# One projection pair of a decoder layer moved behind the memory attention, with its softmax shares per chunk

## Chip, cores and metric

The kernel runs on one core of a Trainium2 chip. The metric is the device time of one execution in microseconds (us), the median of several runs. All computation is in float32; a large product is made of three products of rounded parts (high x high, high x low, low x high).

## What is computed

One layer (DEPTH is 1, so the mixer is the dilated window attention) and a final norm, for x of 2048 x 1024 and 256 memory rows:

```python
h = rmsnorm(x, norm_g[i])
proj = h @ w_in[i]
q, k, v = proj[..., :c1], proj[..., c1:c2], proj[..., c2:c3]
qm, gate = proj[..., c3:c4], proj[..., c4:]
mix = dilated_window_mixer(q, k, v)
mo = memory_attention(qm, rmsnorm(mem, mem_norm_g[i]), w_mem_kv[i])
y = jnp.concatenate([mix, mo], axis=-1) * jax.nn.silu(gate)
x = x + y @ w_out[i]
return rmsnorm(x, final_norm_g)
```

The mixer has three groups of four heads, with windows and dilations (128, 1), (512, 4) and (2048, 16). Each head attends to a band of keys in its own residue class, and the three groups' outputs are weighed against each other, per position and head, by the softmax over the groups of their log-sum-exp. These weights are called shares here. Memory attention has four heads over all 256 memory rows.

## The kernel before

**Staging.** Positions are held in 4 chunks of 512. The normalised input stays in SBUF as a rounded part xH and a remainder xL, [128, chunk, 8, 512] each. In the code group 2 is the one with dilation 16. Heads go in pairs, two heads in 128 rows. The main loop (L755) takes the pairs in the order (2,0), (2,1), (1,0), (1,1), (0,0), (0,1); for each pair and chunk it makes four projections, K, V, Q and gate (`proj_k`, `proj_v`, `proj_q`, `proj_gate`), each 24 matmuls at L140 to L142. At the end of a chunk `burst` (L477) issues the values of the chunk before and the scores of this one. Exponentials come with their row sums (`nm_all`, `l_all`); the weights are turned by a VectorE transposition and a round trip through DRAM (`turn_tiles`, L329: one DMA out at L336, four back at L342). The result times its gate goes to a DRAM buffer (`store_z`).

**After the pairs** `memory_kv` has made the memory keys and values, and eight memory units (pair, chunk) follow (L815 to L828): a Q and a gate projection each, then `mem_values` (L444) of the unit two back and `mem_scores` (L455) of this one. Beside them `shares` (L557) turns the row maxima and sums of all heads, sends them to DRAM (`st_dr`), reads them back with 128 lanes, weighs the groups and writes `f_dr`. From the fourth unit on the output weights are loaded over chunks 0 and 1 of xH and xL (`load_wo`, L607), and from the seventh on y for chunk 0 is made over chunk 2 (`make_y`, L621): load z, load the shares of two heads broadcast over 64 rows each, multiply (L638), round (L639), subtract (L640).

**Output.** `out_block` (L654) multiplies 128 positions by the output weights, 48 matmuls of 512 columns in two banks (L669 to L671), adds the residual rows on eviction (L674), and norms. Sixteen blocks follow each other, and during those of chunk c y for chunk c+1 is made. The last two memory units' values are issued after blocks 0 and 2 (L835).

**Order.** A slot is a step of `run` (L706): a fourth of a projection, six matmuls. `at(n, f)` issues f n slots later; `steps` runs a generator one step for each slot. The framework adds the waits, assigns the buffers of a tag and orders each engine's instructions when the kernel is built, starting from the order of the code; it may take an instruction ahead of others that it reckons not ready. So memory values and scores stand among the projections of later units. All DMAs are issued by SP, in one queue. PSUM has three banks for projections and output (`pp`), four for scores (`ps`) and one for values (`po`).

## Time and profile before

| | us |
|---|---|
| median of 3 runs | 997.66 (996.65 to 997.77) |
| the profiled execution, its own time | 999.34 |
| its span from first to last instruction | 997.4 |
| TensorE busy in the span | 965.4 |
| first matmul of the output stage | 777.67 |

Busy times are those of one profiled execution. A line of the code (L669) names the instruction's place; a tile's name (`pp`, `xH`) what it writes and reads. Where an operation waits, the profile names the instruction that released it. Matmuls are pipelined, so one lasts longer than the step from one to the next.

### The profile page before, as it was taken

Reading aid. Unit: us, or ns where it says so; the run is one execution under the profiler, and the core shown is the slowest. Engines: PE = TensorE matmul, PEld = TensorE weight load, DVE = VectorE, ACT = ScalarE, POOL = GpSimd, SP = SyncE. Lnnn points to the kernel's source line nnn. Section 1 sums busy time; section 2 is a strip of 40 time slices with the busy share of each in tenths; the row PEclk is TensorE's granted clock in tenths of the full one; section 3 lists DMA queues with packets and bytes.
Section 4 is the critical chain, followed back from the end, with each engine's and each line's share of the span. In section 5 each row is a group of like instructions: output and inputs, shape, how many; then the busy total and the mean of one; then the engine's idle time right before and its main releaser. Section 6 shows DMA issues by size and latency. Waiting matters only on the chain.

```text
span 997.4 us, 13857 instructions
## 1 busy us (share of the span) xinstructions
PE 965.4 (97%) x4836; PEld 758.1 (76%) x4836; DVE 425.7 (43%) x995; ACT 325.1 (33%) x992; POOL 245.5 (25%) x391
## 2 busy tenths in 40 slices
PE   8899999999999999999999999999999788999997
PEld 6677888887888888877777777787767466788886
DVE  7866333333333333333334334335543544465333
ACT  5755422242223222332233232433232330232111
POOL 4411500050004100321123011245356450011000
PEclk9999999999999999999999999999999889899999
DMA  6465321141224322442345432534475775887311
GB/s 198 153 201 180 128 74 53 54 146 67 74 86 135 124 80 85 131 135 85 95 117 158 118 93 87 174 131 130 120 211 173 219 224 182 270 244 243 117 64 63
DMA packets 102133, 135.17 MB, mean 136 GB/s; under 512 B 29872, under 2 KB 63920, under 8 KB 102064
## 3 DMA queue, kind: packets, MB, share of 16 engines
q1 hardware_dynamic: 102064, 134.30, 43.0%
q8 instruction: 38, 0.62, 0.3%
q14 instruction: 31, 0.25, 0.1%
HBM read 89.14 MB, written 45.12 MB: 135 GB/s over the span
## 4 chain that ended last, share of the span: by engine, by line
PE 82%; issue 2%; DMA 2%; DVE 1%; POOL 1%; ACT 1%; POOLq 0%; SPq 0%; ACTq 0%
PE pp L140 18%; PE pp L142 18%; PE pp L141 18%; PE pp L669 6%; PE pp L670 6%; PE pp L671 6%; PE ps L399 3%; PE po L421 3%; PE ps L455 1%; PE po L444 1%; DMA p<-t_dr 1%; POOL p L471 1%; PE pp L540 1%; DMA wh<-in_xrows 1%; ACT p L464 1%
## 5 line engine op out<-in xcount | busy, mean ns | idle before, releaser
L140 PE MATMUL pp<-xH,wh 128*128 128x512 f32 x888 | 357.2, 403 | 0.0
L142 PE MATMUL pp<-xH,wl 128*128 128x512 f32 x888 | 353.5, 398 | 1.8 <-DVE wl L78 1.8
L141 PE MATMUL pp<-xL,wh 128*128 128x512 f32 x888 | 353.3, 398 | 1.5 <-DVE xL L198 1.5
L140 PEld LDWEIGHTS pp<-xH,wh 128*128 128x128 f32 x888 | 167.8, 189 | 47.6 <-issue 7.7
L142 PEld LDWEIGHTS pp<-xH,wl 128*128 128x128 f32 x888 | 167.5, 189 | 45.3 <-DVE wl L78 3.5
L141 PEld LDWEIGHTS pp<-xL,wh 128*128 128x128 f32 x888 | 167.7, 189 | 42.5 <-DVE xL L198 2.4
L324 POOL COPY vb<-mid 32x128 f32<-32x128 f32 (+1 forms) x208 | 60.1, 289 | 260.2 <-DVE mid L321 252.0
L669 PE MATMUL pp<-xH 128*128 128x512 f32 (+1 forms) x264 | 105.3, 399 | 11.6 <-ACT xH L639 6.4
L324 ACT COPY vb<-mid 32x128 f32<-32x128 f32 (+1 forms) x208 | 60.7, 292 | 168.8 <-DVE mid L321 166.7
L671 PE MATMUL pp<-xH,xL 128*128 128x512 f32 (+1 forms) x264 | 103.5, 395 | 0.7 <-DVE xL L640 0.7
L670 PE MATMUL pp<-xL,xH 128*128 128x512 f32 (+1 forms) x264 | 104.2, 395 | 0.0
L78 POOL TENSOR_TENSOR wl<-wraw,wh 128x512 fp32r<-128x512 f32 x52 | 67.4, 1308 | 142.1 <-ACT wh L77 136.5
L378 ACT ACTIVATE p<-p,nm_all 128x128 f32<-128x128 f32 (+1 forms) x192 | 86.1, 450 | 44.2 <-DVE nm_all L377 28.5
L333 DVE STREAM_TRANSPOSE mid<-p 128x1024 f32<-128x1024 f32 (+1 forms) x56 | 66.9, 1194 | 49.8 <-DMA t_dr<-mid 33.9
L471 POOL TENSOR_SCALAR p<-p,sm 128x256 f32<-128x256 f32 x64 | 62.8, 1000 | 72.0 <-DVE sm L467 54.9
L310 DVE SCALAR_TENSOR_TENSOR tmp<-pp,Rb 128x512 f32<-128x512 f32 x31 | 21.4, 691 | 121.8 <-PE pp L142 121.7
L669 PEld LDWEIGHTS pp<-xH 128*128 128x128 f32 x264 | 51.3, 194 | 25.4 <-ACT xH L639 8.4
L311 ACT ACTIVATE u<-tmp 128x512 f32<-128x512 f32 x29 | 18.2, 629 | 144.9 <-DVE tmp L310 144.6
L671 PEld LDWEIGHTS pp<-xH,xL 128*128 128x128 f32 x264 | 51.3, 195 | 13.5 <-DVE xL L640 2.4
L377 DVE CUSTOM_DVE_ANT_0 p<-ps,nb 128x128 f32<-128x128 f32 (+1 forms) x192 | 57.5, 362 | 7.8 <-PE ps L399 7.6
L670 PEld LDWEIGHTS pp<-xL,xH 128*128 128x128 f32 x264 | 51.5, 195 | 10.3 <-issue 0.4
L249 DVE TENSOR_TENSOR tmp<-pp,Rb 128x512 f32<-128x512 f32 x24 | 16.6, 691 | 82.0 <-PE pp L142 81.9
(137 smaller groups left out, 839.1 us busy)
## 6 DMA issues: line engine op xcount, KB each, us to landing
t_dr<-mid SPq DMA_DIRECT2D x46, 512.0 KB, 3.0
p<-t_dr SPq DMA_DIRECT2D x184, 128.0 KB, 3.3
wraw<-in_w_in SPq DMA_DIRECT2D x56, 256.0 KB, 2.9
wh<-in_xrows SPq DMA_DIRECT2D x16, 512.0 KB, 5.3
out<-wh SPq DMA_DIRECT2D x15, 512.0 KB, 3.1
z_dr<-u SPq DMA_DIRECT2D x29, 256.0 KB, 2.9
Rb<-z_dr SPq DMA_DIRECT2D x24, 256.0 KB, 5.5
tmp<-in_xT SPq DMA_DIRECT2D x22, 256.0 KB, 3.1
```

Of the source, the lines that this page charges most:

```text
L78: on.tensor_tensor(wl, raw, wh.bitcast(F32), op=ALU.subtract)
L140: pe.matmul(ps, wh[:, k, :], xh, start=(k == 0), stop=False)
L141: pe.matmul(ps, wh[:, k, :], xl, start=False, stop=False)
L142: pe.matmul(ps, wl[:, k, :], xh, start=False, stop=(k == NK - 1))
L324: (gp.tensor_copy if (i + j) % 2 else a.copy)(dst[32 * j:32 * j + 32, :, 32 * i:32 * i + 32], mid[32 * i:32 * i + 32, :, 32 * j:32 * j + 32])
L333: v.transpose(mid.rearrange("p (j t b) -> p t j b", j=4, t=n), src.rearrange("p (t j b) -> p t j b", t=n, j=4))
L377: v.tensor_tensor_reduce(p, sc, bias, -SCALE, BIG, ALU.add, ALU.min, nm)
L378: a.activation(p, p, AF.Exp, bias=nm, scale=-1.0, accum_out=l)
L471: gp.tensor_scalar(w, w, sm[:, 1, h, b:b + 1], None, op0=ALU.mult)
L669: pe.matmul(ps, yH[:, k, bs], woH[:, k, ns], start=(k == 0), stop=False)
L670: pe.matmul(ps, yH[:, k, bs], woL[:, k, ns], start=False, stop=False)
L671: pe.matmul(ps, yL[:, k, bs], woH[:, k, ns], start=False, stop=(k == NK - 1))
```

## The change

The second pair of group 2 is taken out of its place behind the first one and comes after the memory attention (in the list of pairs (3,0) stands for the memory units, whose order is now pair by pair). Its weights are loaded during the last three memory units. `shares` is run beside the memory units for all heads but the two of the moved pair, whose rows of group 2 do not exist yet; `chunk_shares` does the same for heads 2 and 3 (of every group) chunk by chunk, one chunk behind the moved pair, with `weigh_groups` in common and in three steps. The output weights are loaded during chunks 1 and 2 of the moved pair (`load_wo`, one each 1.875 slots), y for chunk 0 during its chunk 3. The last two memory units' values are issued in its chunk 0, at slot 6 and at the end. Residual rows are loaded two blocks ahead instead of one. The shares in `make_y` have two staging buffers instead of three.

```diff
--- before.py
+++ after.py
@@ -60,6 +60,8 @@
 
     gp.memset(ones, 1.0)
     gp.memset(mhalf, -0.5)
+    gp.memset(nm_all[:, 2, 2:], 0.0)
+    gp.memset(l_all[:, 2, 2:], 0.0)
 
     main = ExitStack()
     pool = main.enter_context(tc.tile_pool(name="main", bufs=1))
@@ -554,16 +556,35 @@
         yield
 
 
+    def weigh_groups(m, f):
+
+        v.tensor_tensor(f[:, 3, :], m[:, 0, :], m[:, 2, :], op=ALU.min)
+        v.tensor_tensor(f[:, 3, :], f[:, 3, :], m[:, 4, :], op=ALU.min)
+        for g in range(3):
+            v.tensor_tensor(f[:, g, :], f[:, 3, :], m[:, 2 * g, :], op=ALU.subtract)
+        yield
+        a.activation(f[:, :3, :], f[:, :3, :], AF.Exp)
+        yield
+        for g in range(3):
+            v.tensor_tensor(m[:, 2 * g, :], f[:, g, :], m[:, 2 * g + 1, :], op=ALU.mult)
+        v.tensor_tensor(m[:, 0, :], m[:, 0, :], m[:, 2, :], op=ALU.add)
+        v.tensor_tensor(m[:, 0, :], m[:, 0, :], m[:, 4, :], op=ALU.add)
+        v.reciprocal(m[:, 0, :], m[:, 0, :])
+        for g in range(3):
+            v.tensor_tensor(f[:, g, :], f[:, g, :], m[:, 0, :], op=ALU.mult)
+
     def shares():
+
         kk = sb([P, 5 * P], F32, "kk", 2)
         vb = sb([P, 5, P], F32, "vb", 2)
         for i, src in enumerate((nm_all, l_all)):
             for g in range(3):
+                n = 32 if g == 2 else 64
                 pt = pbank()
-                pe.transpose(pt[:64, :P], src[:, g].rearrange("p h b -> p (h b)"), ident)
+                pe.transpose(pt[:n, :P], src[:, g, :n // 16].rearrange("p h b -> p (h b)"), ident)
                 t = (vb[:64, 3 * i + g, :] if 3 * i + g < 5 else kk[:64, :P])
-                v.tensor_copy(t, pt[:64, :P])
-                for h in range(4):
+                v.tensor_copy(t[:n], pt[:n, :P])
+                for h in range(n // 16):
                     dst = st_dr[2 * g + i, h]
                     s = t[16 * h:16 * h + 16, :]
                     if g == 2:
@@ -576,25 +597,42 @@
                                      s.rearrange("b (r i) -> b r i", r=16))
             yield
         q = S // 32
-        m = kk[:, :6 * q].rearrange("p (s n) -> p s n", s=6)
-        sp.dma_start(m, st_dr.rearrange("s h (b n) -> (h b) s n", n=q))
+        m = kk[:64, :6 * q].rearrange("p (s n) -> p s n", s=6)
+        sp.dma_start(m, st_dr[:, :2].rearrange("s h (b n) -> (h b) s n", n=q))
         for _ in range(4):
             yield
-        f = vb.rearrange("p b n -> p (b n)")[:, :4 * q]
-        f = f.rearrange("p (s n) -> p s n", s=4)
-        v.tensor_tensor(f[:, 3, :], m[:, 0, :], m[:, 2, :], op=ALU.min)
-        v.tensor_tensor(f[:, 3, :], f[:, 3, :], m[:, 4, :], op=ALU.min)
-        for g in range(3):
-            v.tensor_tensor(f[:, g, :], f[:, 3, :], m[:, 2 * g, :], op=ALU.subtract)
-        a.activation(f[:, :3, :], f[:, :3, :], AF.Exp)
-        for g in range(3):
-            v.tensor_tensor(m[:, 2 * g, :], f[:, g, :], m[:, 2 * g + 1, :], op=ALU.mult)
-        v.tensor_tensor(m[:, 0, :], m[:, 0, :], m[:, 2, :], op=ALU.add)
-        v.tensor_tensor(m[:, 0, :], m[:, 0, :], m[:, 4, :], op=ALU.add)
-        v.reciprocal(m[:, 0, :], m[:, 0, :])
-        for g in range(3):
-            v.tensor_tensor(f[:, g, :], f[:, g, :], m[:, 0, :], op=ALU.mult)
-        sp.dma_start(f_dr.rearrange("g h (b n) -> (h b) g n", n=q), f[:, :3, :])
+        f = vb.rearrange("p b n -> p (b n)")[:64, :4 * q].rearrange("p (s n) -> p s n", s=4)
+        yield from weigh_groups(m, f)
+        yield
+        sp.dma_start(f_dr[:, :2].rearrange("g h (b n) -> (h b) g n", n=q), f[:, :3, :])
+        yield
+
+    def chunk_shares(c):
+
+        cs = slice(c * CH, (c + 1) * CH)
+        t = tmp()
+        for i, src in enumerate((nm_all, l_all)):
+            pt = pbank()
+            pe.transpose(pt[:32, :P], src[:, 2, 2:].rearrange("p h b -> p (h b)"), ident)
+            v.tensor_copy(t[:32, i * P:(i + 1) * P], pt[:32, :P])
+        yield
+        for i in range(2):
+            for h in range(2):
+                b = 16 * h + 4 * c
+                sp.dma_start(st_dr[4 + i, 2 + h, cs].rearrange("(r n) -> r n", r=4), t[b:b + 4, i * P:(i + 1) * P])
+        q = CH // 32
+        m = t[:64, 2 * P:2 * P + 6 * q].rearrange("p (s n) -> p s n", s=6)
+        f = t[:64, 3 * P:3 * P + 4 * q].rearrange("p (s n) -> p s n", s=4)
+        for _ in range(2):
+            yield
+        for h in range(2):
+            sp.dma_start(m[32 * h:32 * h + 32], st_dr[:, 2 + h, cs].rearrange("s (b n) -> b s n", n=q))
+        for _ in range(3):
+            yield
+        yield from weigh_groups(m, f)
+        yield
+        for h in range(2):
+            sp.dma_start(f_dr[:, 2 + h, cs].rearrange("g (b n) -> b g n", n=q), f[32 * h:32 * h + 32, :3, :])
         yield
 
 
@@ -624,10 +662,9 @@
         cs = slice(c * CH, (c + 1) * CH)
         if not staged:
             kk = sb([P, 5 * P], F32, "kk", 2)
-            vb = sb([P, 5, P], F32, "vb", 2).rearrange("p b n -> p (b n)")
-            staged.append([Rb[:, i * CH:(i + 1) * CH] for i in range(3)] + [vb[:, :CH]])
-            staged.append([sb([P, CH], F32, "wraw", 2), sb([P, CH], F32, "wraw", 2), kk[:, :CH]])
-        t, f = staged[0][k % 4], staged[1][k % 3]
+            staged.append([Rb[:, i * CH:(i + 1) * CH] for i in range(3)] + [kk[:, :CH]])
+            staged.append([sb([P, CH], F32, "wraw", 2) for _ in range(2)])
+        t, f = staged[0][k % 4], staged[1][k % 2]
         sp.dma_start(t, z_dr[k // 2][:, k % 2, cs])
         if k < 6:
             for h in range(2):
@@ -657,8 +694,8 @@
         bs = slice(b * P, (b + 1) * P)
         x_t = residual.pop(r)
         last = r == 15
-        if not last:
-            at(3, lambda: load_rows(r + 1))
+        if r < 14:
+            at(3, lambda: load_rows(r + 2))
         cuts = (0, 512, 768, 1024) if last else (0, 512, 1024)
         ss = sb([P, 6], F32, "ss", 2)
         sq = row_tile("wl")
@@ -751,8 +788,30 @@
 
     mem = {}
     ws = []
-    pairs = [(2, 0), (2, 1), (1, 0), (1, 1), (0, 0), (0, 1)]
+    pairs = [(2, 0), (1, 0), (1, 1), (0, 0), (0, 1), (3, 0), (2, 1)]
+
+    def memory_stage():
+
+        at(20, lambda: steps(shares()))
+        following = []
+        for n in range(8):
+            pp, c = divmod(n, 4)
+            st = {}
+            if n in (5, 6):
+                at(1, lambda t=(11, 17)[n - 5]: following.append(load_w(w_in[t])))
+            run(proj_q(st, 3, c, ws[2 + 2 * pp]))
+            if n == 7:
+                following.append(load_w(w_in[5]))
+            run(proj_gate(st, 3, c, ws[1 + 2 * pp], "nb" if n % 3 == 2 else "u"))
+            if n == 7:
+                following.append(load_w(w_in[25]))
+            burst((st, 3, pp, c), 2)
+        return following
+
     for idx, (g, pp) in enumerate(pairs):
+        if g == 3:
+            ws = memory_stage()
+            continue
         col = 2 * g + pp
         nbs = {}
 
@@ -774,7 +833,7 @@
         else:
             at(7, load_bias)
         following = []
-        if idx < 5:
+        if idx < 4:
             n = 2 * pairs[idx + 1][0] + pairs[idx + 1][1]
             ahead = [6 + n, 12 + n, n, 20 + n]
         else:
@@ -783,9 +842,22 @@
         for c in range(NC):
             st = {}
             pv = prev if g == 0 else None
+            if idx == 6:
+                if c == 0:
+                    at(6, burst)
+                else:
+                    at(3, lambda c=c: steps(chunk_shares(c - 1)))
+                if c == 1:
+                    for i in range(2 * NK):
+                        at(15 * i // 8, lambda i=i: load_wo(i))
+                elif c == 3:
+                    for k in range(NK):
+                        at(2 * k, lambda k=k: make_y(0, k))
+                    for i, fn in ((6, lambda: load_rows(0)), (10, load_gfin), (11, lambda: load_rows(1))):
+                        at(i, fn)
 
             def load_ahead():
-                if c == NC - 1:
+                if c == NC - 1 and idx < 5:
                     t = ahead[len(following)]
                     following.append(load_w(w_in[t]) if t is not None else None)
 
@@ -797,9 +869,9 @@
                     at(14, lambda c=c: spread_r(c + 1))
                     at(17, lambda c=c: spread_r(c + 1))
                 run(proj_k(st, g, c, ws[0], pv, late=4 if (idx, c) == (0, 1) else 0))
-                if (idx, c) == (5, 3):
+                if (idx, c) == (4, 3):
                     steps(memory_kv(mem))
-                elif (idx, c) == (5, 1):
+                elif (idx, c) == (4, 1):
                     steps(memory_squares(mem))
                 load_ahead()
                 run(proj_v(st, g, c, ws[1], pv))
@@ -811,28 +883,14 @@
             burst((st, g, pp, c), 1, nbs[0])
             prev = st
         ws = following
-    at(20, lambda: steps(shares()))
-    for n, (pp, c) in enumerate(((0, 0), (0, 1), (1, 0), (1, 1), (0, 2), (1, 2), (0, 3), (1, 3))):
-        st = {}
-        if n == 3:
-            for i in range(2 * NK):
-                at(4 * i // 3, lambda i=i: load_wo(i))
-        elif n == 6:
-            for k in range(NK):
-                at(2 * k, lambda k=k: make_y(0, k))
-        elif n == 7:
-            at(3, lambda: load_rows(0))
-            at(5, load_gfin)
-        run(proj_q(st, 3, c, ws[2 + 2 * pp]))
-        run(proj_gate(st, 3, c, ws[1 + 2 * pp], "nb" if n % 3 == 1 else "u"))
-        burst((st, 3, pp, c), 2)
+    at(2, lambda: steps(chunk_shares(3)))
     for c in range(NC):
         for b in range(4):
             if c < NC - 1:
                 for i in range(2):
                     at(1 + 3 * i, lambda k=2 * b + i: make_y(c + 1, k))
             run(out_block(c, b))
-            if c == 0 and b in (0, 2):
+            if (c, b) == (0, 0):
                 burst()
     assert not todo, todo
     main.close()
```

## Rows read from the trace of the kernel before

**Rows 1.** The page: busy us by engine; TensorE's share in 40 slices

```profile
PE 965.4 (97%) x4836; PEld 758.1 (76%) x4836; DVE 425.7 (43%) x995; ACT 325.1 (33%) x992; POOL 245.5 (25%) x391
...
PE   8899999999999999999999999999999788999997
```

**Rows 2.** Windows: us; busy (count) of PE, PEld, DVE, ACT, POOL; clock; DMA; GB/s

```profile
765.40:800.00 34.60, 28.45 (x118) 18.46 (x117) 18.11 (x28) 11.13 (x38) 19.33 (x19) 0.83 0.78 219
800.00:825.00 25.00, 21.21 (x88) 15.38 (x88) 11.31 (x20) 8.41 (x24) 11.13 (x10) 0.89 0.76 239
825.00:876.00 51.00, 45.30 (x199) 34.32 (x199) 23.60 (x43) 9.23 (x16) 5.09 (x7) 0.93 0.72 223
876.00:984.00 108.00, 108.00 (x478) 89.41 (x478) 48.66 (x95) 20.49 (x35) 10.67 (x14) 1.00 0.47 152
```

**Rows 3.** Windows, line 669 alone: us; busy (count) of PE, PEld

```profile
777.67:869.94 92.27, 35.44 (x80) 16.84 (x81) 0.87 0.73 224
869.94:978.74 108.80, 62.24 (x160) 30.03 (x160) 1.00 0.52 165
```

**Rows 4.** Windows, line 444 alone, then line 455 alone

```profile
777.67:869.94 92.27, 8.67 (x64) 3.88 (x64) 0.87 0.73 224
697.00:765.40 68.40, 7.19 (x56) 3.09 (x52) 1.00 0.53 157
...
777.67:869.94 92.27, 4.51 (x17) 2.65 (x16) 0.87 0.73 224
697.00:765.40 68.40, 10.76 (x64) 7.04 (x64) 1.00 0.53 157
```

**Rows 5.** Timeline of PE: start, us, form, count [idle before <- releaser]

```profile
776.13 1.58 PE L455 MATMUL ps<-kk,q 64*128 64x256 f32 x8 [1.63 <-ACT p L464]
```

**Rows 6.** Waits of PE over the span: us in total, times, longest

```profile
PE pp L669 <- ACT xH L639: 6.4, 3, 3.6
PE pp L669 <- DVE wh L674: 5.1, 2, 4.9
PE ps L455 <- ACT p L464: 3.3, 2, 1.6
```

**Rows 7.** The chain that ended last, 836 to 850 us: start, us, what

```profile
839.67 1.25 DVE mid L333
...
841.79 6.23 DMA wh<-in_xrows
```

**Rows 8.** Windows of the moved pair's present place, all engines

```profile
192.83:217.45 24.62, 24.62 (x130) 19.84 (x132) 7.70 (x24) 10.02 (x32) 9.93 (x14) 1.00 0.35 118
sum 98.56, PE 98.56 PEld 79.25 DVE 30.80 ACT 29.64 POOL 19.62; mean PE 24.64 PEld 19.81 DVE 7.70 ACT 7.41 POOL 4.90
```

**Rows 9.** Lines 640 and 585: count, ns least/median/most, first and last start

```profile
L640 DVE TENSOR_TENSOR xL<-Rb,xH x24: 680/686/694, 777.9 to 923.0; 128x512 fp32r<-128x512 f32 x24
...
L585 DVE TENSOR_TENSOR vb<-kk x1: 216/216/216, 714.9 to 714.9; 128x64 f32<-128x64 f32 x1
```

**Rows 10.** Line 634, the same columns: issues on SP's queue

```profile
L634 SPq DMA_DIRECT2D wraw<-f_dr x32: 444/530/1438, 764.0 to 912.8; - x32
```

**Rows 11.** DMA issues: count, KB each, median us from issue to landing

```profile
p<-t_dr SPq DMA_DIRECT2D x184, 128.0 KB, 3.3
...
Rb<-z_dr SPq DMA_DIRECT2D x24, 256.0 KB, 5.5
...
wraw<-f_dr SPq DMA_DIRECT2D x32, 128.0 KB, 5.1
...
kk<-st_dr SPq DMA_DIRECT2D x1, 192.0 KB, 4.5
```

**Rows 12.** Timeline of PE: transpositions of the shares

```profile
692.38 0.38 PE L563 MATMUL pp<-ident,nm_all 128*64 128x128 f32 x2
...
694.20 0.30 PE L563 MATMUL pp<-ident,nm_all 128*64 128x128 f32 x1 [0.51 <-DVE vb L565]
```

## Prediction made before the changed kernel was run

> **What bounds the kernel now.** I read the busy table and the 40 slices first [rows 1]. TensorE is busy 97% of the span, so only work it doesn't do, or does slowly, can be saved. The slices show where that is: the first, those between about 775 and 875 us, and the tail after the last matmul. The change touches the second place alone. I then read windows across it [rows 2]. From 876 to 984 us TensorE is busy all the time at a granted clock of 1.00 (2.4 GHz). From 765.4 to 876 us it is idle for 6.15 + 3.79 + 5.70 = 15.6 us, and the clock is granted in part at 1.2 GHz (means 0.83, 0.89 and 0.93).
>
> Idle time alone understates the loss, since a matmul at 1.2 GHz counts as busy for longer. So I counted work. Line 669 starts a third of the output matmuls: 160 of them take 108.80 us where nothing waits, 0.680 us for each triple, but 80 of them took 92.27 us before that [rows 3]. Those 80 triples are worth 54.4 us. In the same stretch lie memory values (64 records) and scores (17). In the memory stage, where nothing waits, such records take 7.19/56 = 0.128 us and 10.76/64 = 0.168 us [rows 4]: 8.2 + 2.9 = 11.1 us. What is left, 92.27 - 54.4 - 11.1 = 26.8 us, is lost. With the 1.63 us gap just ahead of it [rows 5] the loss is **28.4 us**. By idle time it would be 15.6 + 0. The Trainium skill (Perfetto Trace Analysis, "Identifying the Most-Contended Engine") says that matmul busy share is no good measure of headroom on TensorE; by the 15.6 us the sum below would end near 987 us, by the counted loss where it does. The pieces at 1.2 GHz side with the page.
>
> Then the waits: who ended these gaps? The rounded y (6.4 us), the eviction of an output bank (5.1 us), the exponentials of the memory scores (3.3 us) [rows 6]. The chain shows what stands behind the longest one: VectorE turns a memory half at 839.67, SP sends it off, and only then come, in SP's queue, an output store and at 841.79 the load of residual rows, 6.23 us, for which the eviction waits [rows 7]. So one cause feeds several waits: the last memory units run inside the output stage and put their steps ahead of y and of the rows on VectorE, ScalarE and SP, while TensorE has nothing else left that is independent.
>
> **The change, part by part.** Moved: the second pair of group 2, 4 chunks of 24.6 us, 98.56 us in all with TensorE busy 98.56 us [rows 8]. It needs the same matmuls in its new place, so the move costs 0 as long as weights, bias and buffers come in time. Weights are loaded 12 or more slots ahead, as now (a slot is 24.6/16 = 1.54 us, so 18 us).
>
> What it gives: output weights are loaded in its chunks 1 and 2, y of chunk 0 in its chunk 3, and the last memory units end in its chunks 0 and 1. There VectorE is busy 7.7 of 24.6 us and the DMA engines 35% even where the next weights are loaded [rows 8]. TensorE then has independent projections while a memory unit is on its way. Residual rows are asked for two blocks ahead instead of one, so the 6.23 us landing has a block of 16 triples more, 10.9 us. Full removal is **-28.4 us**.
>
> What comes back or is added:
>
> Chunk 3 of the moved pair. Besides its own steps it holds 8 z loads, 12 share broadcasts, the rows, and VectorE gets 4 products and 8 subtractions at 0.69 us plus the shares of chunk 2, 16 operations of some 0.22 us [rows 9]. VectorE: 7.7 + 12 x 0.69 + 16 x 0.22 = 19.5 of 24.6 us. SP: 20 x 0.53 for z and shares and some 14 more at about that price [rows 10], 18 of 24.6 us. Both fit, yet z and shares land 5.5 and 5.1 us after issue [rows 11] while the product is queued 2 slots, 3.1 us, after it. VectorE waits behind that, and the next evictions of projections wait behind VectorE. The cover is three PSUM banks of 5.6 us each, about 10 us. Lower end 0 (from 876 us on the same pattern of y and output costs nothing [rows 2]); upper end 10 us, worked out below as a rival. I take **+3**, nearer to the lower end because the nearest row is the undisturbed output stage.
>
> Shares per chunk. Eight transpositions on TensorE: two of those now there took 0.38 us beside their neighbours, a third waited 0.51 us for its bank [rows 12]. Between 0 and 4 x (0.38 + 0.51) = 3.6 us; I take **+1**, since a bank is waited for once in three. Their chain of a write, a read (4.5 us for the whole table [rows 11]) and a write back lies in one chunk of 24.6 us, and its result is wanted a chunk later or more. If that cover is gone, each weighing holds up VectorE; that is the slower rival. The former single weighing loses only its 64 added lanes, worth nothing. The Exp on ScalarE comes four times more, off the path.
>
> Flushed memory unit. The seventh unit's values are called 6 slots into chunk 0, which leaves 1 slot rather than 3 between the issue of its turned weights and their use. The landing is 3.3 us [rows 11], so up to 3.3 - 1.5 = 1.8 us are uncovered, 0 if projections are put ahead. I take **+1**. On SP the waits of the weight loads, bias and halves stand in one queue there, but the halves are not wanted again for a chunk.
>
> Two small memsets at the start lie on GpSimd before anything waits for it: 0. One staging buffer fewer for the shares (2 instead of 3), and y tile 3 in a key buffer: a load of y k+2 waits for product k, which is 2 slots earlier: 0 where products are on time, and inside the +3 where not. The load of rows two ahead needs a third buffer of four: 0.
>
> Sum: -28.4 + 3 + 1 + 1 = **-23.4 us**. The profiled execution took 999.34 us (span 997.4), so 975.9 there; the three times before have a median of 997.66, 1.7 lower, which gives 974.3, rounded to **975**.
>
> **Rivals.**
>
> A, the forecast: stalls of the output stage go, a few us come back in the last chunk. 969 to 981 us; 969 is the full 28.4 us.
>
> B, the last chunk becomes the bound. VectorE holds 19.5 us of work in chunk 3 and waits 4 times for 5.5 - 3.1 = 2.4 us at its own products: 29.1 us against 24.6. It overruns by 4.5 us, y arrives late in the first output block, TensorE pauses and its clock falls; before, 15.6 us of idle cost 28.4, so 4.5 us cost 8.2, and with the late rows behind it on SP 10 to 12. About 984 us (981 to 988). For it: high shares on SP and VectorE, and the 6.23 us landing at 841.79 shows how a queue passes lateness on [rows 7]. Against it: no wait from 876 us on with half that density. The Trainium skill (Perfetto Trace Analysis, "What 'DMA-bound' means") counts an issuing sequencer that is solid with DMA slices as a bound of its own; the 18 us of 24.6 reckoned from rows stay under that, so the page alone would not make B happen.
>
> C, the stage doesn't lose its waits, because they belong to y and the rows rather than to the memory units. Of 15.6 us idle, 6.4 + 5.1 = 11.5 stand at line 669 [rows 6]. If that part stays, 28.4 x 11.5/15.6 = 20.9 us stay and 7.5 go, less 1 added: 991 us. Against it: the chain above, in which both follow a memory unit.
>
> D, slower. The weighing per chunk stops VectorE in its queue until the small DMAs land, four times. It decides once VectorE stands longer than the 10 us of PSUM cover plus 23.4/4 = 5.9 us for each chunk, that is a read that lands 4.6 + 16 = 20 us after issue; measured is 4.5 us, for runs four times as long [rows 11]. At 22 us it would be 975 + 4 x 8 = 1007 us. The Trainium skill (DMA: Bandwidth & Descriptors, "Specifications") gives 512 B as the least size for full rate; the new reads have runs of 64 B, but only 384 per chunk, and no run here shows such reads yet.
>
> **How the numbers follow.** A 0.64, B 0.21, C 0.07, D 0.05, and 0.03 that so much comes back that nothing is left to measure. About 0.2% is what a measurement of this kernel can tell from no change. Faster: A, B and C, 0.92; within 0.2%: 0.03; slower: 0.05. The likeliest is A, 975. For 8 in 10 the range takes A and most of B: 969 to 986.
>
> **What would show it.** Right: in the windows, the first output blocks run at 0.680 us a triple and a clock of 1.00; line 669's waits on y and rows together under 3 us; SP loads residual rows a block early. The +3 is seen as waits of projections or of the first output block in the last 25 us before the output stage. The +1 of shares is seen at the transposition's line. B shows as VectorE near full in that chunk and a granted clock below 1 there; C as waits at line 669 as large as now; D as VectorE waiting for the read of the shares. The forecast is wrong if the matmuls of the moved pair take longer in the new place than 24.6 us a chunk, or if the memory stage, which now has nothing of the output in it, does not hold its pace.

## The result, and the profile of the changed kernel

The changed kernel takes **991.38 us** (median of 6, 990.45 to 994.75) against 997.71 us (996.65 to 1000.26) before in the same job: ratio 0.994 [0.9918, 0.9962]. It is faster, by 6.3 us; the forecast was 975 and its range ended at 986. The profiled execution took 994.41 us with a span of 992.3 us, 5.1 us under the span before. One execution of no_chunk_shares below (3057.25 us; its other three 976.92 to 979.34) was disturbed and is left out of every time and ratio here.

The page, as in [rows 1]: busy us by engine, and TensorE's share in 40 slices of 24.8 us.

```profile
PE 961.4 (97%) x4844; PEld 755.5 (76%) x4844; DVE 436.8 (44%) x1059; ACT 326.0 (33%) x996; POOL 242.6 (24%) x393
...
PE   7899999999999999999999999999969999999997
```

The weak stretch of [rows 1] near 775 to 875 us is gone, and one slice with a 6 has appeared, at 719 to 744 us. The windows of [rows 2] over the kernel after:

```profile
765.40:800.00 34.60, 32.87 (x166) 26.21 (x165) 19.43 (x60) 13.61 (x43) 10.26 (x19) 1.00 0.55 164
800.00:825.00 25.00, 24.75 (x128) 19.34 (x127) 14.57 (x49) 8.53 (x26) 3.22 (x5) 1.00 0.74 229
825.00:876.00 51.00, 50.96 (x235) 41.63 (x234) 29.20 (x63) 10.75 (x19) 6.16 (x7) 1.00 0.66 205
876.00:984.00 108.00, 108.00 (x496) 90.23 (x495) 46.34 (x91) 20.66 (x37) 10.39 (x13) 1.00 0.42 136
```

Idle time there was 15.6 us and is 2.0 us; the clock is 1.00 throughout. The output stage now starts at 807.9 us. The first part of its line that starts triples (706 here, 669 in [rows 3]), from there to the same 869.94 us:

```profile
807.90:869.94 62.04, 33.94 (x88) 16.54 (x88) 1.00 0.67 212
869.94:978.74 108.80, 62.30 (x161) 30.04 (x160) 1.00 0.44 141
```

By the count of the forecast, 88 triples at 0.680 us are 59.8 us; the remaining 2.2 us hold values, scores and two transpositions. So hardly anything is lost where 28.4 us were.

What was lost instead stands in the stretch before. Windows of the kernel after:

```profile
700.00:720.00 20.00, 20.00 (x103) 14.87 (x102) 7.13 (x11) 6.96 (x22) 9.17 (x10) 1.00 0.48 157
720.00:740.00 20.00, 11.15 (x48) 7.51 (x46) 8.49 (x25) 7.92 (x28) 9.11 (x14) 0.77 0.63 204
740.00:805.00 65.00, 61.95 (x316) 47.98 (x315) 30.33 (x93) 22.13 (x72) 15.58 (x30) 0.99 0.50 148
```

From 720 to 740 us TensorE did 48 matmuls where it did 103 in the 20 us ahead: 20 x (1 - 48/103) = 10.7 us lost at one place, 8.85 us of it idle, the rest at the half clock. Some 3 us more lie idle up to 805 us. TensorE's waits from 590 us on (us in total, times, longest), to be read against [rows 6]:

```profile
PE pp L616 <- DVE nm_all L379: 5.4, 1, 5.4
PE pp L616 <- DVE kk L251: 3.1, 2, 1.7
PE po L446 <- POOL xL L653: 2.8, 1, 2.8
PE pp L584 <- DVE vb L586: 2.1, 1, 2.1
PE pp L616 <- ACT p L380: 0.7, 1, 0.7
PE pp L706 <- ACT xH L676: 0.2, 1, 0.2
```

Line 616 is the transposition of the chunk shares, new with this change: 9.2 of the 14.3 us stand there, and 0.2 us at the output matmuls. The 2.1 us at L584 are the transposition of `shares` in the memory stage. From 590 to 700 us this execution has 507 matmul records where tr_late, tr_late_out and no_shares_again have 521 or 522, about 3 us, and it took 3.0 us more than the median; whether its other executions lost anything there no trace shows. The timeline of TensorE at the first of these transpositions (start, us, form; idle before and its releaser), which answers to [rows 5, 12]:

```profile
728.81 1.08 PE L446 MATMUL po<-p,vb 128*64 128x256 f32 x8 [2.77 <-POOL xL L653]
735.31 0.40 PE L616 MATMUL pp<-ident,nm_all 128*32 128x128 f32 x1 [5.42 <-DVE nm_all L379]
736.37 0.40 PE L616 MATMUL pp<-ident,l_all 128*32 128x128 f32 x1 [0.66 <-ACT p L380]
736.42 0.78 PE L142 MATMUL pp<-xH,wh 128*128 128x512 f32 x1
```

The transposition takes 0.4 us, as in [rows 12], but it waits until VectorE has weighed the last block of the moved pair's first chunk (L379 adds the bias to the scores and takes the row maxima). The projection behind it needs nothing of that, and starts 0.05 us after the second transposition. The Trainium skill (PSUM — Partial Sum Buffer, "Engine vs sequencer instructions") says that matmuls start and complete in program order; these four lines agree.

Why was the weighing late? SP's queue and then VectorE's, in order of time:

```profile
701.34 0.38 SPq L338 DMA_DIRECT2D t_dr<-mid  x1
711.94 0.35 SPq L649 DMA_DIRECT2D Rb<-in_w_out  x1
...
713.52 1.79 SPq L344 DMA_DIRECT2D p<-t_dr  x4
...
721.78 0.33 SPq L649 DMA_DIRECT2D Rb<-in_w_out  x1
...
723.46 1.79 SPq L344 DMA_DIRECT2D p<-t_dr  x4
725.30 0.43 SPq L338 DMA_DIRECT2D t_dr<-mid  x1
725.78 0.43 SPq L820 DMA_DIRECT2D nb<-in_nbias  x1
```

```profile
729.92 0.71 DVE L323 STREAM_TRANSPOSE mid<-tmp 128x512 f32<-128x512 f32 x1 [8.38 <-DMA t_dr<-mid]
730.56 0.65 DVE L426 TENSOR_TENSOR u<-u,po 128x512 f32<-128x512 f32 x1
731.13 0.28 DVE L379 CUSTOM_DVE_ANT_0 p<-ps,nb 128x128 f32<-128x128 f32 x1
```

SP stands 10.1 us (to 711.94) at a load of output weights (L649) into a piece of Rb that the moved pair's first gate still reads; the return of a turned memory half (L344) is queued behind it. It stands again, to 721.78, at the next such load. A later half leaves only at 725.30, VectorE stands 8.38 us for the single buffer `mid`, through which it next shifts the moved pair's values V (L323), and behind that stands L379. The pair's bias is issued at 725.78 as well: its buffer `nb` held the gate of memory unit 5.

### The profile page after: what moved, and what is told of

Same layout as the page of the kernel before. It is cut to its first block, busy times and chain, and to the rows that moved or that the text cites. A ratio compares the mean times of both kernels' runs of the same rounds, so it can differ in the third digit from the quotient of the medians.

```text
span 992.3 us, 13998 instructions
## 1 busy us (share of the span) xinstructions
PE 961.4 (97%) x4844; PEld 755.5 (76%) x4844; DVE 436.8 (44%) x1059; ACT 326.0 (33%) x996; POOL 242.6 (24%) x393
## 5 line engine op out<-in xcount | busy, mean ns | idle before, releaser
L706 PE MATMUL pp<-xH 128*128 128x512 f32 (+1 forms) x264 | 101.1, 384 | 0.2 <-ACT xH L676 0.2
L707 PE MATMUL pp<-xL,xH 128*128 128x512 f32 (+1 forms) x264 | 101.0, 383 | 0.0
L708 PE MATMUL pp<-xH,xL 128*128 128x512 f32 (+1 forms) x264 | 100.9, 384 | 0.0
L380 ACT ACTIVATE p<-p,nm_all 128x128 f32<-128x128 f32 (+1 forms) x192 | 86.2, 450 | 43.3 <-DVE nm_all L379 27.4
L473 POOL TENSOR_SCALAR p<-p,sm 128x256 f32<-128x256 f32 x64 | 58.2, 928 | 77.5 <-DVE sm L469 77.5
L379 DVE CUSTOM_DVE_ANT_0 p<-ps,nb 128x128 f32<-128x128 f32 (+1 forms) x192 | 58.0, 360 | 7.8 <-PE ps L401 7.6
L708 PEld LDWEIGHTS pp<-xH,xL 128*128 128x128 f32 x264 | 49.6, 188 | 10.4 <-DVE xL L677 0.5
L706 PEld LDWEIGHTS pp<-xH 128*128 128x128 f32 x264 | 49.7, 188 | 10.1 <-ACT xH L676 0.4
L466 ACT ACTIVATE p<-ps,sm 128x256 f32<-128x256 f32 x64 | 29.5, 476 | 82.5 <-issue 46.6
```

The costliest lines, as they stand in the source:

```text
L379: v.tensor_tensor_reduce(p, sc, bias, -SCALE, BIG, ALU.add, ALU.min, nm)
L380: a.activation(p, p, AF.Exp, bias=nm, scale=-1.0, accum_out=l)
L473: gp.tensor_scalar(w, w, sm[:, 1, h, b:b + 1], None, op0=ALU.mult)
L706: pe.matmul(ps, yH[:, k, bs], woH[:, k, ns], start=(k == 0), stop=False)
L707: pe.matmul(ps, yH[:, k, bs], woL[:, k, ns], start=False, stop=False)
L708: pe.matmul(ps, yL[:, k, bs], woH[:, k, ns], start=False, stop=(k == NK - 1))
```

## The experiments

The theories. **T**: the transpositions of the chunk shares stand too early in TensorE's queue. **Q**: loads of output weights put ahead of the halves' return on SP make VectorE late. **B**: the late bias does. **M**: the single `mid` does. **Y**: the values of output chunk 0 come late on their own. All ratios are to the kernel before, run in the same job.

### One cause at a time, by a later slot

wo_late loads the output weights in chunk 2, one a slot (its last piece is overwritten before it is rounded); tr_late calls the chunk shares at slot 9; both_late does both; no_wo leaves the loads of output weights out.

```diff
-                if c == 1:
+                if c == 2:
...
-                        at(15 * i // 8, lambda i=i: load_wo(i))
+                        at(i, lambda i=i: load_wo(i))
```

```diff
-                    at(3, lambda c=c: steps(chunk_shares(c - 1)))
+                    at(9, lambda c=c: steps(chunk_shares(c - 1)))
```

Expected of wo_late: 

> The changed kernel (991.4 us) with one edit: all 16 loads of the output weights start in chunk 2 of the moved pair, one each slot, instead of from chunk 1 on at one in 1.875 slots. Theory Q (queue): in the changed kernel a load of output weights into Rb stands on SP from 701.7 to 711.9 us, waiting for the last eviction that reads that part of Rb, with the return of a turned memory half behind it; everything late between 719 and 745 us follows from that. Q expects the 11 us lost there to go: 979 to 983 us, and the 5.4 us wait at the transposition of the chunk shares to go with them although that transposition is not moved. Theory T (transpositions): the eight transpositions stand too early in TensorE's queue and wait for the scores' maxima whatever SP does. T expects 989 to 992 us and the waits at the transposition as before (9 us).

Of tr_late: 

> The changed kernel (991.4 us) with one edit: the chunk shares of the moved pair start 9 slots into the next chunk instead of 3, so their transpositions stand later in TensorE's queue. Theory Q (a load of output weights blocks SP's queue): the late memory halves and the 8.4 us in which VectorE waits for the one transposition buffer stay, only the waits at the transposition (9.2 us in three places) are partly covered by projections: 985 to 990 us. Theory T (transpositions stand too early by themselves): 979 to 983 us, with the first values of the stretch no longer late.

Of both_late: 

> Both edits: output weights in chunk 2 of the moved pair and chunk shares 9 slots into a chunk. If Q and T each hold a part, this is the best of the three, 974 to 979 us; if Q alone holds, it is as wo_late, within 2 us; if T alone holds, as tr_late, within 2 us.

Of no_wo: 

> The changed kernel without any load of output weights: the 16 loads, their 16 roundings and 16 subtractions are left out, and the output matmuls run on what lies in their buffers. It bounds what these loads cost in all. Theory Q: as low as wo_late or up to 4 us lower (977 to 982 us), since what wo_late moves is gone here. Theory T: 988 to 992 us.

Measured: wo_late 988.55 us, 0.990 [0.9883, 0.9917]; tr_late 988.45, 0.9903 [0.9885, 0.9922]; both_late 993.54, 0.9951 [0.9933, 0.9969]; no_wo 983.57, 0.9858 [0.9836, 0.9881]. Of these only tr_late lies in a named range, that of Q (985 to 990 us); wo_late lies just under T's, no_wo between the two, both_late in none. In wo_late SP still stands 10.1 us at L649. In tr_late the wait at the transposition is as long as it was:

```profile
736.86 0.40 PE L616 MATMUL pp<-ident,nm_all 128*32 128x128 f32 x1 [5.61 <-DVE nm_all L379]
```

The order on each engine is set by the planner when the kernel is built; a slot only shifts when a step is traced. So wo_late did not test Q. In tr_late the transposition did move: it stands 72 projection matmuls behind the chunk's scores, where the kernel after has 48. But VectorE's weighing slid as well: its last block ends 29 us after the scores started (707.67 us), in the kernel after 24 us after them. A later place alone was thus not enough there, against T as it was put. In no_wo SP stands 10 us all the same, at a load of values into Rb: the loads of output weights are not needed for that wait. Taking them away gives 7.8 us, and TensorE still waits 3.6 us at the transposition.

### What makes VectorE late (Q, B, M)

own_bias gives the moved pair's bias a tile of 1 KB a partition and loads it in the memory stage. wo_behind orders loads of output weights and values on SP behind the half returned last. own_behind has both; own_behind_tmp also shifts values V through the common scratch buffers, so that `mid` serves the turned halves alone. That edit is in `shift_tiles`, which the memory's values and those of every pair go through; L323 at 729.92 above is of the moved pair.

```diff
+            ownb.append(sb([P, 2, P], F32, "nb2", 1))
+            sp.dma_start(ownb[0], nbias[5][:, :, P:])
```

```diff
+                returned[0] = sp.dma_start(rows, d.rearrange("(i a) (j t b) -> j a i t b", i=4, j=4, t=n)[j]).ins
...
+        with tc.issue_after(returned[0]):
+            sp.dma_start(raw, w_out[:, k, ns])
```

```diff
-        mid = sb([P, 8 * P], F32, "mid", 1)[:, :n * P].rearrange("p (t n) -> p t n", t=n)
+        mid = tmp()[:, :n * P].rearrange("p (t n) -> p t n", t=n)
```

Expected of own_bias: 

> The changed kernel with one edit: the moved pair's bias (only its own half, 1 KB a partition) gets a tile of its own and is loaded in the memory attention, so that it no longer waits for the store of memory unit 5, whose gate has the shared buffer. Theory B (the late bias holds the weighing of the moved pair's first chunk, and through it the queue of VectorE and the transposition of the shares on TensorE): the 5.4 us wait of TensorE at about 730 us goes, 985 to 987 us. Theory Q (SP stands 10.1 us at about 702 us on a load of output weights that waits for a piece of Rb, and the memory halves' return behind it is late): the wait stays at 4 to 6 us, 990 to 992 us.

Of wo_behind: 

> The changed kernel with one edit: on SP the loads of output weights, and those of values for the output, are ordered behind the return of the half turned last before them, so none of them can stand ahead of a memory half. Theory Q: SP's 10.1 us at 702 us and VectorE's 8.4 us on the turned half go, and the transposition's wait falls from 5.4 us to under 2: 984 to 987 us. Theory B: the halves come earlier, but the weighing still waits for its bias, issued at about 720 us: the wait falls by 1 to 3 us, 988 to 990 us.

Of own_behind: 

> Both edits at once: own tile for the bias, and loads of output weights and values behind the halves' return. If B and Q each carry a part of the loss of about 11 us between 720 and 740 us, it nearly goes: 980 to 984 us. If either is enough alone, the time is that of the better single one. If neither is the cause (single buffer of the turned halves, theory M), a wait of 3 to 6 us at 730 us remains: 988 to 991 us.

Of own_behind_tmp: 

> The two edits, and the shifted memory values go through the common scratch buffers in place of the single buffer through which halves are turned. Theory M (VectorE stands in its queue for that one buffer): 1 to 3 us less than with the two edits alone, 978 to 982 us. If the buffer of the halves isn't what VectorE waits for by then: within 1 us of the two edits alone.

Measured: own_bias 993.84 us, 0.9949 [0.9932, 0.9965]; wo_behind 989.42, 0.9905 [0.9886, 0.9924]; own_behind 999.25, 1.0006 [0.9996, 1.0017]; own_behind_tmp 990.78, 0.9918 [0.9896, 0.9939]. Only wo_behind lies in a range that had been named (988 to 990 us, for B); own_bias, which should have confirmed B, doesn't, and the two sums are far off. But the traces are telling. The window at 720 us of own_bias, then of wo_behind:

```profile
720.00:740.00 20.00, 16.53 (x73) 11.75 (x72) 7.31 (x24) 6.68 (x26) 5.12 (x11) 0.91 0.34 106
```

```profile
720.00:740.00 20.00, 15.87 (x70) 10.22 (x69) 7.95 (x25) 7.40 (x27) 4.84 (x10) 0.83 0.57 188
```

Each single edit gives back 22 to 25 of the 55 matmuls missing there; own_bias loses it again from 790 to 815 us (93 matmuls). The windows of own_behind_tmp at 720 and 790 us, and its longest wait:

```profile
720.00:740.00 20.00, 20.00 (x104) 14.70 (x104) 6.77 (x13) 2.03 (x8) 0.00 (x0) 1.00 0.51 171
...
790.00:815.00 25.00, 18.24 (x83) 12.29 (x82) 13.01 (x46) 8.27 (x27) 3.20 (x4) 0.82 0.66 195
```

```profile
PE pp L709 <- ACT xH L679: 5.3, 3, 2.9
```

With the halves, the bias and `mid` out of the way the loss at 720 us is gone in full: the weighing ends 9 us after the scores started, where it was 24 us in the kernel after, 17 in own_bias and 19 in wo_behind. So Q, B and M together do name what made the weighing late. But the time is the same. The output stage starts earlier (791.9 us, not 807.9), its first matmuls wait 5.3 us for rounded y (L679), where the kernel after waited 0.2, and the clock falls there. And 3.1 us are lost at the transposition of `shares` near 599 us; own_cs_def, own_cs_pool and own_tr_behind_def, which have the same edit of `shift_tiles`, lose 2.9 to 3.1 us there too, the other edited kernels that do the changed kernel's whole work 0.3 or 0.4. Why own_behind, with one edit less, loses still more (8 us idle from 790 to 840 us) I can't say: each edit also reorders the rest.

### The chunk shares at the end (Y)

cs_def makes the shares of chunks 2 and 3 in the output stage; own_cs_def does that on top of own_behind_tmp; own_cs_pool instead issues the shares' small transfers on GpSimd's queue.

```diff
-                else:
+                elif c < 3:
                     at(3, lambda c=c: steps(chunk_shares(c - 1)))
...
-    at(2, lambda: steps(chunk_shares(3)))
+    at(2, lambda: steps(chunk_shares(2)))
+    at(14, lambda: steps(chunk_shares(3)))
```

Expected of cs_def: 

> The changed kernel with one edit: the shares of the moved pair's chunk 2 are made in the output stage (traced from its slot 2), those of chunk 3 from slot 14, instead of chunk 2's inside chunk 3. If theory Y holds (the values of output chunk 0 are made too late because SP and VectorE stand on chunk 2's weighing, so whatever is saved before 790 us is lost again at 790 to 815 us), the wait at 788 to 810 us goes and the time is 986 to 989 us, the 11 us at 730 staying. If the values' own pace is what counts: 990 to 992 us.

Of own_cs_def: 

> own_behind_tmp (no loss left at 720 to 750 us, but some 13 us at 790 to 815 us) with the shares of chunks 2 and 3 moved into the output stage. Theory Y: the values of output chunk 0 come in time and the loss at 790 to 815 us falls to under 4 us: 977 to 982 us. If the values are late by their own work on VectorE and ScalarE: 987 to 991 us.

Of own_cs_pool: 

> own_behind_tmp with the small transfers of the chunk shares (stores of sums, their gathering, stores of weights) issued on the queue of GpSimd in place of SP's. If SP's queue, in which the loads of values stand behind these transfers (6 us at 805 us), is what makes the values late: 977 to 983 us. If it is VectorE's order: within 2 us of own_behind_tmp's 990.8 us. If GpSimd's issue of them stands in the way of its own work: up to 5 us slower than that.

Measured: cs_def 992.9 us, 0.9942 [0.9923, 0.9961]; own_cs_def 985.58, 0.9867 [0.9851, 0.9884]; own_cs_pool 996.17, 0.9977 [0.9965, 0.9989]. Alone, moving chunk 2's shares gives nothing; the loss at 720 us stays (52 matmuls in that window). Where that is gone, it gives 5.2 us, about half of what Y had said; the wait for y falls from 5.3 to 3.0 us. With the small transfers off SP's queue the kernel loses 5 us, the third branch named, at transpositions again (5.8 and 5.5 us); GpSimd is busy 15.6 us from 765 to 790 us, 11.0 in own_behind_tmp. That doesn't clear SP's queue, since GpSimd's own price may hide a gain.

### The price of the chunk shares, and which part of them has it (T)

no_chunk_shares leaves the moved pair's shares out and makes the shares of all heads in the memory stage, with zeros in the pair's place; no_shares_again is the same kernel, run again for its trace. tr_only puts the transpositions and the copies out of PSUM back in their early place, and leaves out the weighing, its transfers and stores. tr_behind calls the shares at slot 16 instead of 3 and orders the transpositions behind gate matmuls of the next chunk; tr_behind_def has the shares of chunks 2 and 3 in the output stage besides; own_tr_behind_def adds the three edits of own_behind_tmp; tr_late_out is tr_behind_def with chunk 2's and 3's transpositions also ordered, behind output matmuls (slots 9 and 24).

```diff
-        pe.matmul(ps, wl[:, k, :], xh, start=False, stop=(k == NK - 1))
+        pe_last[0] = pe.matmul(ps, wl[:, k, :], xh, start=False, stop=(k == NK - 1)).ins
...
-                    at(3, lambda c=c: steps(chunk_shares(c - 1)))
+                    at(16, lambda c=c: steps(chunk_shares(c - 1)))
...
+            with tc.issue_after(pe_last[0]):
                 pe.transpose(pt[:32, :P], src[:, 2, 2:].rearrange("p h b -> p (h b)"), ident)
```

Expected of no_chunk_shares: 

> The changed kernel without the shares of the moved pair's chunks: their transpositions, weighings and small transfers are left out, and the shares of all heads are made in the memory attention, with zeros in the place of the moved pair's (so its weights in the output are not the true ones). Theory T (the transpositions on TensorE, at which it stood at 594, 730, 760, 788 and 810 us, and the queues behind them, carry nearly all of the 16 to 20 us given back): 974 to 979 us. Theories Q and B (late halves and late bias, the transposition only shows them): the late halves stop TensorE at the next values instead, 984 to 988 us.

Of no_shares_again: 

> The kernel without the shares of the moved pair's chunks once more (they are left out; the pair's weights in the output are not the true ones), for its profile: 977 to 979 us as before. Theory T: no wait of TensorE over 2 us between 700 and 830 us. Theory Q: a wait of 3 to 6 us at 720 to 740 us at the values of a memory half.

Of tr_behind: 

> The changed kernel with one edit: the transpositions of the moved pair's chunk shares are ordered behind matmuls of the next chunk's gate projection in TensorE's queue, some 16 us later than the profile of the changed kernel has them. Theory T (they stand too early in the queue: TensorE waits there for a weighing that nothing hurries): the wait of 5.4 us at 730 us and those at 760 and 788 us go, 980 to 984 us. Theory Q (what is late is VectorE and the halves, and TensorE would stand at the next values or projections instead): 988 to 991 us.

Of tr_behind_def: 

> As tr_behind, with the shares of chunks 2 and 3 made in the output stage. If the values of output chunk 0 become the next bound once the transpositions stand later (theory Y), this gives 2 to 4 us over tr_behind: 977 to 981 us. If not: within 1 us of tr_behind.

Of own_tr_behind_def: 

> As tr_behind_def, with the moved pair's bias in its own tile, the loads of output weights and values ordered behind the halves' return, and the memory values shifted through the scratch buffers. If each of these takes a wait of its own: 975 to 979 us. If the place of the transpositions is what mattered and the rest only reorders: within 2 us of tr_behind_def. Against own_cs_def's 985.6 us, which has the transpositions early, it shows the worth of their place alone.

Of tr_only: 

> The changed kernel with the moved pair's transpositions and their copies out of PSUM in their early place, and nothing behind them: the weighing, its small transfers and the stores of its weights are left out (shares of all heads as in no_chunk_shares, so the output's weights are not the true ones). Theory T: TensorE still waits 4 to 6 us at 725 to 735 us, 984 to 989 us against 977 to 978 without the transpositions. If the weighing and the transfers on VectorE's and SP's queues carry the price: 977 to 980 us.

Of tr_late_out: 

> As tr_behind_def, with the transpositions for chunk 2 ordered behind output matmuls of the first output blocks, those for chunk 3 after them. Theory T: the 6.4 us lost at 790 to 800 us go, 977 to 980 us. If the loss there is the values of output chunk 0 (theory Y): within 1 us of tr_behind_def's 984.0 us.

Measured: no_chunk_shares 977.02 us, 0.9785 [0.9766, 0.9805], and again 976.68, 0.9787 [0.9766, 0.9808]. The shares cost 14.4 and 14.7 us by these medians, 15.3 to 15.5 by the ratios of each job. Without them the late halves stop nothing: the windows of no_shares_again are full at both places, and no wait of TensorE stands between 700 and 860 us.

```profile
720.00:740.00 20.00, 20.00 (x104) 14.84 (x103) 6.03 (x20) 4.59 (x15) 7.00 (x12) 1.00 0.47 145
...
790.00:815.00 25.00, 24.89 (x118) 19.21 (x117) 14.40 (x37) 9.43 (x26) 3.15 (x3) 1.00 0.97 278
```

tr_only: 991.17 us, 0.9916 [0.9898, 0.9934], the median of the changed kernel; by the ratios it is 2.4 us faster, with intervals that overlap. The transpositions in their early place are enough for nearly the whole price; weighing, transfers and stores have little or no part in it. Its window and its waits:

```profile
720.00:740.00 20.00, 10.01 (x45) 6.51 (x45) 7.98 (x25) 7.88 (x29) 10.83 (x17) 0.77 0.67 221
```

```profile
PE pp L616 <- DVE nm_all L379: 4.8, 1, 4.8
PE po L446 <- POOL xL L635: 4.6, 1, 4.6
```

One reserve: with the transposition there, the planner also sets the memory values (L446) closer together, at 725.75 and 731.42 us, and the second waits too; without it they start at 723.3 and 734.1 us. The runs don't part the wait at the transposition from that order around it.

tr_behind: 986.48 us, 0.9887 [0.9871, 0.9903]; tr_behind_def 983.99, 0.9861 [0.9843, 0.9878]; own_tr_behind_def 987.29, 0.9894 [0.9878, 0.9911]; tr_late_out **980.98, 0.9829 [0.9805, 0.9853]**. A later place, with all work done, gives 4.9, then 7.4, then 10.4 us over the changed kernel; the last two also make the shares of two chunks in the output stage. tr_late_out beats both kernels. Of the ranges of T, that of no_chunk_shares came out and tr_late_out is 1 us above its own; tr_behind lies between those of T and Q, tr_only and tr_behind_def outside those named. Its windows and its waits from 700 to 860 us:

```profile
720.00:740.00 20.00, 19.99 (x102) 14.49 (x101) 7.55 (x35) 7.27 (x28) 4.89 (x10) 1.00 0.51 161
740.00:765.00 25.00, 24.61 (x135) 18.48 (x136) 11.63 (x34) 10.48 (x41) 6.60 (x11) 1.00 0.46 149
765.00:790.00 25.00, 25.00 (x130) 19.78 (x131) 15.30 (x35) 9.85 (x27) 8.90 (x13) 1.00 0.61 182
790.00:815.00 25.00, 22.88 (x108) 16.76 (x107) 16.91 (x53) 10.83 (x33) 5.53 (x10) 1.00 0.94 280
```

```profile
PE pp L709 <- ACT xH L679: 3.7, 4, 1.6
PE pp L619 <- DVE nm_all L381: 0.4, 1, 0.4
```

At the transposition (L619 here) 0.4 us are left of 9.2. In tr_behind the first transposition stands 113 projection matmuls behind the chunk's scores. SP still stands 10.1 us at its load there, the weighing of that chunk ends later than in the kernel after (31 us behind the scores), and nothing is lost at 720 us: once the projections don't stand behind the weighing on TensorE, the late halves cost nothing there. No run has slot 16 without the explicit order, so which of the two moved the transposition is open.

Adding the edits against Q, B and M then makes it slower by 3.3 us (own_tr_behind_def, in none of its ranges); near 599 us it waits 2.8 us longer. By the medians of two jobs it is also 1.7 us slower than own_cs_def, its twin with the transpositions early. In that pair, in which the first weighing is in time, the later place gained nothing.

## Why the prediction was wrong, by its own steps

**The loss counted in the output stage, and its removal (-28.4): right.** Windows, waits and triples show next to nothing left of it.

**Residual rows two blocks ahead (counted into the 28.4): right as far as it shows.** The 5.1 us of [rows 6] at the eviction are gone from TensorE's waits. That part was not tried alone.

**Chunk 3 (+3) and the flushed memory unit (+1): near in sum, not shown where they were put.** Without chunk shares the profiled span is 974.5 us, 22.9 under the span before; the forecast less its shares term is -24.4. The two terms and whatever else is left thus come to 5.5 us where 4 were taken, and to 7.5 by the medians of that job (997.56 and 976.68). But that trace has no wait at either place. The wait for y, for which the +3 stands, is 0.2 us in the kernel after, 3.7 in tr_late_out, 5.3 in own_behind_tmp and nothing in no_shares_again, whose output stage starts as early (788.9 us) as that of tr_late_out (788.7): it takes the work of the chunk shares as well. The cover behind its upper end was misreckoned: three banks of 5.6 us are 16.8 us, not about 10. For the +1, bounded by 1.8, the kernel after shows 2.8 us: the wait of 2.77 at L446 is the seventh unit's second half. The profile names a subtraction (L653) there; at the same wait of wo_late and cs_def, 1.3 and 2.6 us, it names the half's return.

**Shares per chunk (+1, bounds 0 to 3.6): this step failed.** It cost 14 to 15 us. I had named the transposition's line as the place to look, and the waits are there, but I priced the transposition by its own 0.38 us and by the wait for a PSUM bank, from a row of the old place [rows 12], where the sums had long been there. In the new place its input is the end of the moved pair's weighing, 20 to 24 us after its scores (711 us), through a queue of VectorE that also serves the halves, the bias and the evictions; and what is queued behind it on TensorE is all the rest. That input (L379, L380) has 6.1 of the 9.2 us; the other 3.1, at two later transpositions, end with an eviction (L251), the wait for a bank that I had at 0.51 and that was up to 1.7. The forecast asked of each added wait on VectorE and SP what stands behind it, and not of this one on TensorE. Its cover of a whole chunk was right for the use of the shares and was never there for the transposition.

**Rival D, slower by the weighing's small reads: refuted.** The kernel is faster, its trace has no wait of VectorE for that read, and tr_only, which has no such reads, has the same median.

**Rival C, 991 us: its number came out and its reason didn't.** The waits for y and rows went from 11.5 to 0.2 us.

**SP's one queue (in the part on the flushed unit): wrong.** I wrote that the halves are not wanted again for a chunk. The seventh unit's second half was wanted in that chunk, as just said, and the buffer `mid` was, by VectorE, 8.38 us. In tr_behind, where SP stands as long, neither shows as a wait of TensorE at 720 us, so both mattered together with the transposition's place.

## What to carry to other kernels

A cheap instruction put into the queue of the engine that sets the time costs what its input is late by, and, as here, the fall of the clock after it; so price it by the tail of its producer's queue in the new place, not by its own duration in the old one. Where a planner orders the engines, see in the trace whether it stands behind independent work, and order it there if it doesn't: here an explicit order, with a slot 13 later and two chunks' shares in the output stage, was worth 10.4 us, while a slot 6 later left the wait as it was. A wait removed ahead of another limit can return there; look at which wait is next before counting the gain.

## What the runs showed that I had not expected

Edits that each lowered the time, or part of the loss at 720 us, did not add up: 988.55 and 988.45 us singly gave 993.54 together, and 993.84 and 989.42 gave 999.25. An idle stretch of 8.85 us cost 10.7 us of work, since the granted clock fell to 1.2 GHz for some matmuls after it (0.43 us from one to the next where it was 0.23; a mean of 0.77 from 720 to 740 us); without the shares the clock stayed at 1.00 there.
